# A hybrid decoder layer: the preparation and inverse of a block's delta rule moved into its own input projection

## The chip, the cores and the metric

One core of a Trainium2 chip runs the whole layer. The time is device microseconds (us) of one execution; the kernel before took 2666.4 us (median of three runs, 2665.94 to 2672.2).

## The reference

`x` is 2048 tokens of 1024 float32 channels; 16 meta tokens stand ahead of them. One layer:

```python
h = rmsnorm(x, norm1_g);  proj = h @ w_in            # 3608 columns: q, k, v, gates, decays
# four delta-rule heads (dk = dv = 128), after a causal conv of 4 taps, silu and l2norm of q and k:
a = (k * beta) @ k.T * decay;  m = I + strict_lower(a)
u, w = solve(m, v * beta), solve(m, k * beta * exp(gc))
v_new = u - w @ S;  o = (q * exp(gc)) @ S + (q @ k.T * decay) @ v_new
S = S * exp(gc[-1]) + (k * exp(gc[-1] - gc)).T @ v_new   # state, from chunk to chunk
# four GLA heads (dk = 64, dv = 128): the same with a decay per channel and no solve
o = rmsnorm(o) * silu(gate)                          # both groups
x = x + concat(o_dn, o_gla) @ w_out
x = x + square(relu(rmsnorm(x, norm2_g) @ w_up)) @ w_down;  out = rmsnorm(x, final_norm_g)
```

## The kernel before, in words

Products are made in float32 as three products of rounded halves (`mm3`, L117 to L120: high x high, low x high, high x low), into PSUM banks of 128 x 512. The tokens come in four blocks of 512 (`b` = 0 to 3), each of four chunks of 128 for the scan.

The program has these parts, in the order it is written:

- `phase_a(b)`: the input projection of block b, eight groups of four banks named `pa`, 96 matmuls for each group and pass over the banks: first a token group (`wtk[0]`: decays and the first part of GLA's values), three convolution groups (k, q, v), the GLA q and k group, and three token groups (values and gates). VectorE evacuates, makes the convolution (`cy`), the gates (`gth`) and the polynomial of log1p. Results go to DRAM (`qkv_d`, `gate_d`, `gla_d`, `gcr_d`).
- `scan_block(b)`: for the four chunks `dn_pre` (transposes of k and q, norms, `kdt`, `U`, `at`), then `dn_inverse` of the four `U` together: the 32 x 32 blocks on the diagonal go through DRAM (`inv_u`) into one tile `inv_v` of 64 partitions, 60 VectorE instructions invert them, and they go back the same way. Then for each chunk `gla`, `dn_levels` (the inverse of the whole 128 x 128 from its diagonal, matmuls `pr`, `pp`) and `dn_rec` (the delta rule proper, `pv`, `pks`, `py`, `po`, `pu`); `flush_mix` transposes results (`pmix`) and stores them in `mix_d`. A chunk's chain goes back and forth between PE and VectorE, each step on the one before; the state `S` links the chunks.
- `wo_block(b)`, in `tail_part`: the output projection of a block, two halves of four banks `pc`, 192 matmuls; residual, a sum of squares on GpSimd (`tot`), and `token_scale` (`pf`, `pfb`), whose result the norm uses at once.
- `layer1`, `layer2`: the MLP, two blocks at a time, by a Strassen scheme of seven products (`p`).

The order of the instructions on each engine is set by a scheduler at build time, which takes the parts' order in the program as priority and lets later parts fill an engine. So `phase_a(b + 1)` fills PE while `scan_block(b)` runs, and the output projections fill it during the last scan. `tc.high_priority(offset=n)` puts instructions n places earlier in that priority. Each engine then runs its own queue in order; a wait of an instruction holds all behind it. All transfers are issued on SyncE (SP), in order too. Tiles of a tag share `bufs` buffers in turn. Of the page's names, `b`, `x` and `tot` are the output projections' tiles.

The lines that set the order of the scan:

```python
scan_meta()
for b in range(NB):
    if b + 1 == NB:
        wstack.close()
    scan_block(b)
    if b + 1 < NB:
        phase_a(b + 1, ka)
tail_part(kc)
```

## Time and profile before

| what | value |
|---|---|
| runs | 2665.94, 2666.4, 2672.2 us |
| profiled execution | 2671.58 us, span of its instructions 2668.7 us |
| mean granted clock of PE | 0.959 |
| PE busy | 2464.6 us, 92% |
| VectorE (DVE) busy | 1871.9 us, 70% |
| ScalarE (ACT) busy | 1147.0 us, 43% |
| GpSimd (POOL) busy | 536.3 us, 20% |
| last input projection matmul starts | 919.2 us into the span |
| first MLP matmul starts | 1308.4 us |

Busy is the union of an engine's instructions. Matmuls overlap, so a busy PE can still be slowed: the granted clock says so, 1.00 being full speed and 0.50 half. The bracket at the end of a timeline row says how long the engine was idle before the instruction and what ended it. The row of a window has the time in which each engine was busy, with the number of its instructions.

### The profile page before, as it was taken

To read this page: it belongs to the slowest core of one execution; us is meant where nothing else is said; L and a number is where in the kernel's file an instruction comes from. 1 tells how busy PE (TensorE), PEld (TensorE's weight loads), DVE (VectorE), ACT (ScalarE), POOL (GpSimd) and SP (SyncE) were. 2 spreads that over 40 slices of the span, in tenths; PEclk is the share of its full clock that TensorE was granted. 3 is DMA by queue.
4 is the path that set the end of the run, shared out by engine and by line. 5 is a ranking of instruction groups with operands and counts; after the bars stand their busy time and mean duration, and the time that the engine had idled before them with its cause. 6 is when DMAs were issued, how large, how long until landed. Compare 5 with 4: busy or idle time off the path is not lost.

```text
span 2668.7 us, 36615 instructions
## 1 busy us (share of the span) xinstructions
PE 2464.6 (92%) x12810; PEld 2029.9 (76%) x12810; DVE 1871.9 (70%) x3377; ACT 1147.0 (43%) x2241; POOL 536.3 (20%) x408
## 2 busy tenths in 40 slices
PE   8998899989998999685999999999969999899997
PEld 6788688868877877574788887778757888788776
DVE  4776896796589676856576666677778666557765
ACT  4345345533444444333354544433354454444433
POOL 2124233342333223231111110000111111100002
PEclk9999999999999999796999999999989999999999
DMA  5266355535645584461444447567527444656644
GB/s 178 95 205 200 110 191 178 179 132 167 188 129 178 169 273 144 142 190 52 142 157 144 143 156 285 188 215 231 165 81 266 148 157 144 209 187 210 214 135 137
DMA packets 292304, 454.73 MB, mean 170 GB/s; under 512 B 44544, under 2 KB 147544, under 8 KB 292120
## 3 DMA queue, kind: packets, MB, share of 16 engines
q1 hardware_dynamic: 292120, 452.41, 52.6%
q8 instruction: 100, 1.64, 0.2%
q14 instruction: 84, 0.69, 0.1%
HBM read 329.58 MB, written 122.72 MB: 169 GB/s over the span
## 4 chain that ended last, share of the span: by engine, by line
PE 66%; DVE 18%; DMA 8%; issue 3%; ACT 2%; POOL 2%; SPq 1%; DVEq 0%; POOLq 0%; ACTq 0%
PE p L119 15%; PE p L118 15%; PE p L120 15%; PE pa L118 3%; PE pa L119 3%; PE pa L120 3%; DVE cy L425 2%; PE pc L118 1%; PE pc L119 1%; PE pc L120 1%; DVE wlo L103 1%; DVE inv_v L575 1%; DMA gcb<-gcr_d 1%; DVE inv_t L569 1%; DMA gl<-gla_d 1%
## 5 line engine op out<-in xcount | busy, mean ns | idle before, releaser
L119 PE MATMUL p<-bl,w7h 128*128 128x512 f32 x832 | 322.7, 398 | 8.4 <-DVE bl L967 8.3
L120 PE MATMUL p<-bh,w7l 128*128 128x512 f32 x832 | 319.9, 399 | 0.0
L966 ACT CAST w7h<-s 128x1024 fp32r<-128x1024 f32 (+1 forms) x128 | 120.6, 942 | 347.4 <-PE p L119 293.0
L102 ACT CAST whi<-wraw 128x1024 fp32r<-128x1024 f32 (+1 forms) x160 | 154.7, 967 | 241.4 <-PE pa L120 79.3
L118 PE MATMUL p<-bh,w7h 128*128 128x512 f32 x832 | 228.9, 403 | 14.5 <-ACT bh L966 12.4
L880 POOL TENSOR_TENSOR tot<-tot,sqk 128x512 f32<-128x512 f32 (+1 forms) x56 | 79.2, 1414 | 734.5 <-ACT sqk L879 725.7
L103 POOL TENSOR_TENSOR wlo<-wraw,whi 128x780 fp32r<-128x780 f32 (+1 forms) x64 | 147.2, 2301 | 361.4 <-ACT whi L102 265.5
L118 PE MATMUL pa<-hh,whi 128*128 128x512 f32 x512 | 208.7, 408 | 4.9 <-ACT whi L102 2.6
L119 PE MATMUL pa<-hl,whi 128*128 128x512 f32 x512 | 206.2, 403 | 0.0
L967 DVE TENSOR_TENSOR w7l<-s,w7h 128x1024 fp32r<-128x1024 f32 (+1 forms) x128 | 140.6, 1098 | 93.1 <-ACT w7h L966 88.4
L120 PE MATMUL pa<-hh,wlo 128*128 128x512 f32 x512 | 194.4, 404 | 9.6 <-POOL wlo L103 8.2
L118 PEld LDWEIGHTS p<-bh,w7h 128*128 128x128 f32 x832 | 159.7, 192 | 54.8 <-ACT bh L966 13.5
L967 DVE TENSOR_TENSOR w7l<-w,w7h 128x1024 fp32r<-128x1024 f32 (+1 forms) x96 | 102.1, 1063 | 134.7 <-ACT w7h L966 134.3
L119 PEld LDWEIGHTS p<-bl,w7h 128*128 128x128 f32 x832 | 158.1, 190 | 47.5 <-DVE bl L967 10.4
L120 PEld LDWEIGHTS p<-bh,w7l 128*128 128x128 f32 x832 | 157.4, 189 | 39.3
L119 PE MATMUL pa<-wlo,hh 128*128 128x390 f32 x512 | 180.4, 355 | 3.2 <-POOL wlo L103 1.9
L118 PE MATMUL pa<-whi,hh 128*128 128x390 f32 x512 | 167.6, 357 | 14.5 <-ACT hh L113 9.9
L120 PE MATMUL pa<-whi,hl 128*128 128x390 f32 x512 | 174.1, 348 | 0.5 <-DVE hl L114 0.5
L967 DVE TENSOR_TENSOR bl<-br,bh 128x1024 fp32r<-128x1024 f32 (+2 forms) x144 | 148.2, 1031 | 35.1 <-ACT bh L966 35.1
L966 ACT CAST bh<-br 128x1024 fp32r<-128x1024 f32 (+2 forms) x144 | 123.7, 859 | 87.6 <-PE p L120 49.3
L103 DVE TENSOR_TENSOR wlo<-wraw,whi 128x1024 fp32r<-128x1024 f32 (+1 forms) x96 | 113.9, 1186 | 67.0 <-ACT whi L102 66.7
L1067 POOL TENSOR_TENSOR q<-r 128x512 f32<-128x512 f32 x32 | 57.7, 1803 | 495.7 <-ACT r L1066 452.2
(381 smaller groups left out, 6197.5 us busy)
## 6 DMA issues: line engine op xcount, KB each, us to landing
br<-sq_d SPq DMA_DIRECT2D x208, 256.0 KB, 3.6
w<-in_dn_dram SPq DMA_DIRECT2D x96, 512.0 KB, 4.7
wraw<-in_wch_dram SPq DMA_DIRECT2D x64, 512.0 KB, 3.6
w<-in_up_dram SPq DMA_DIRECT2D x64, 512.0 KB, 3.7
sq_d<-q SPq DMA_DIRECT2D x128, 256.0 KB, 2.3
wraw<-in_wtk_dram SPq DMA_DIRECT2D x64, 390.0 KB, 3.9
sq_d<-c SPq DMA_DIRECT2D x96, 256.0 KB, 2.8
wraw<-in_wo_dram SPq DMA_DIRECT2D x32, 512.0 KB, 4.1
```

What stands on the lines that cost most here:

```text
L102: A.copy(out=hi[:, :, 0:n], in_=raw[:, :, 0:n])
L103: eng.tensor_tensor(out=lo[:, :, 0:n], in0=raw[:, :, 0:n], in1=hi[:, :, 0:n].bitcast(F32), op=ALU.subtract)
L118: T.matmul(o, lhsT=ah, rhs=bh, start=first, stop=False)
L119: T.matmul(o, lhsT=ah, rhs=bl, start=False, stop=False)
L120: T.matmul(o, lhsT=al, rhs=bh, start=False, stop=last)
L425: V.scalar_tensor_tensor(out=y, in0=raw[:, q : q + TB], scalar=convw[:, m, q : q + 1], in1=y, op0=ALU.mult, op1=ALU.add)
L569: V.tensor_tensor(out=t, in0=vv[:, 0:c, c : c + 1].broadcast_to([L, c, n]), in1=vv[:, c : c + 1, c + 1 : w].broadcast_to([L, c, n]), op=AL ...
L575: V.tensor_tensor(out=vv[:, 0:c, c + 1 : w], in0=vv[:, 0:c, c + 1 : w], in1=t, op=ALU.add)
L880: eng.tensor_tensor(out=tot, in0=tot, in1=sq, op=ALU.add)
L966: A.copy(out=hi, in_=x)
L967: V.tensor_tensor(out=lo, in0=x, in1=hi.bitcast(F32), op=ALU.subtract)
L1067: G.tensor_tensor(out=q12, in0=u, in1=r5, op=ALU.add)
```

## The change

- A new function `ahead(b, also)` makes a block's four `dn_pre` and its `dn_inverse`, at a high priority; `phase_a(b)` calls it (`mid`) after its three convolution groups, before its last four groups. With b > 0 the last chunk (`scan_chunk(b - 1, 3)`) of the block before goes with it. The other three chunks stand ahead of `phase_a(b)`; block 3's four chunks come after it.
- `kdt`, `U` and `at` of all chunks go to DRAM when made (three shared buffers, tag `pre`), and are loaded for their chunk. `dn_inverse` reads its diagonal blocks from `u_d` in DRAM straight into `inv_v` and writes them back there.
- log1p of the delta rule's decays (`whole`) is made in one go, not in steps between the projection's groups.
- In the output projections the sums of squares are added on VectorE, and `token_scale` of a block is made between the two halves of the next block (`between`), of the last block in the first group of `layer1`.

The order the scheduler makes, at three places. PE, from the last matmul of the third output block (`pc`) to the first of the fourth, before (`py` to `pmix` are the delta rule of a chunk, `pr5` starts one):

```order
L120 MATMUL pc_12128<-mxh_11970,wlo_12222 128x512
L669 MATMUL py_10458<-nkv_10444,U_9976 128x128 x4
L679 MATMUL pu_10474<-vs_10463,kdt_9963 128x128 x4
L597 MATMUL pr5_10610<-wt_10606,U_10045 32x32 x8
L679 MATMUL pu_10688<-vs_10677,kdt_10032 128x128 x4
L597 MATMUL pr5_10824<-wt_10820,U_10114 32x32 x8
L679 MATMUL pu_10902<-vs_10891,kdt_10101 128x128 x4
L597 MATMUL pr5_11038<-wt_11034,U_10183 32x32 x8
L679 MATMUL pu_11116<-vs_11105,kdt_10170 128x128 x4
L821 MATMUL pmix_11150<-ident_69,mix_11033 128x128 x4
L118 MATMUL pc_12351<-mxh_12304,whi_12357 128x512
```

The same place on PE in the changed kernel:

```order
L120 MATMUL pc_12307<-mxh_12117,wlo_12401 128x512
L610 MATMUL pr5_11209<-wt_11205,U_11203 32x32 x8
L685 MATMUL py_11275<-nkv_11261,U_11203 128x128 x4
L695 MATMUL pu_11291<-vs_11280,kdt_11253 128x128 x4
L837 MATMUL pmix_11325<-ident_69,mix_11202 128x128 x4
L118 MATMUL pc_12505<-mxh_12458,whi_12511 128x512
```

(Rows between those shown are left out.) Four delta rules, the first in its second half, stood between the two blocks; now one does. The first delta rule of block 3 starts after 192 of the 768 `pc` matmuls, the second after 324, the third after 466.

PE where the sum of squares of the second output block is used, before:

```order
L120 MATMUL pc_11751<-mxh_11597,wlo_11845 128x512
L856 MATMUL pf_11896<-ones_70,tot_11601 128x1 x4
L871 MATMUL pfb_11905<-dg_11906,ones_70 128x128
L118 MATMUL pc_11975<-mxh_11928,whi_11981 128x512
L119 MATMUL pc_11975<-mxl_11929,whi_11981 128x512
```

The sum of the same block in the changed kernel, in the middle of the third block (`pp5`, `pr6` to `pks` are a chunk's delta rule):

```order
L120 MATMUL pc_12125<-mxh_12117,wlo_12219 128x512
L867 MATMUL pf_12273<-ones_70,tot_11746 128x1 x3
L630 MATMUL pr6_11016<-wt_10985,U_10983 64x64 x4
L681 MATMUL pks_11049<-S_182,kg_11045 128x128 x4
L882 MATMUL pfb_12282<-dg_12283,ones_70 128x128
L118 MATMUL pc_12304<-mxh_12075,whi_12310 128x512
```

`pf` and `pfb` stood between two blocks, right behind the last sum; now 96 `pc` matmuls lie between, with scan work around them.

VectorE amid the inverse (`inv_t`, `inv_v`) of the second block, before:

```order
L167 SCALAR_TENSOR_TENSOR l1p_6430<-l1p_6430,gle_6427 128x512
L425 SCALAR_TENSOR_TENSOR cy_6434<-craw_6412,convw_147,cy_6434 128x512
L569 TENSOR_TENSOR inv_t_4931<-inv_v_4930 64x238
L575 TENSOR_TENSOR inv_v_4930<-inv_v_4930,inv_t_4931 64x17x14
L569 TENSOR_TENSOR inv_t_4931<-inv_v_4930 64x240
L575 TENSOR_TENSOR inv_v_4930<-inv_v_4930,inv_t_4931 64x16x15
```

The inverse of the same block in the changed kernel:

```order
L635 COPY U_4357<-pp6_4396 64x4x64
L589 TENSOR_TENSOR inv_v_4164<-inv_v_4164,inv_t_4165 64x19x12
L671 TENSOR_TENSOR nkv_4415<-pv_4410,nkh_1473 128x512
L583 TENSOR_TENSOR inv_t_4165<-inv_v_4164 64x234
L358 SCALAR_TENSOR_TENSOR gth_5086<-gth_5086,tok_5072 128x390
L682 TENSOR_TENSOR nkv_4415<-nkv_4415,pks_4423 128x512
L589 TENSOR_TENSOR inv_v_4164<-inv_v_4164,inv_t_4165 64x18x13
L687 TENSOR_TENSOR vs_4434<-py_4429,brk2_1476 128x512
```

The inverse stood among the convolution and log1p of the next block's projection; now it stands among the gates of its own and the delta rule of the last chunk before.

The diff, cut to its core:

```diff
+    u_d, at_d, kdt_d = [[dp.tile([128, 4, 128], F32, name=f"{n}_d{c}") for c in range(NCH)] for n in ("u", "at", "kdt")]
+    u_m = dp.tile([NMETA, 4, NMETA], F32, name="u_m")
...
-    def phase_a(b, kc, late=None):
+    def phase_a(b, kc, late=None, mid=None):
...
+        def whole(job):
+            try:
+                while True:
+                    next(job)
+            except StopIteration as end:
+                return end.value
...
-            l = yield from log1p(e[:p], p, [nt, 4], f"l1p_s{nt}")
+            l = whole(log1p(e[:p], p, [nt, 4], f"l1p_s{nt}"))
...
+        mid()
...
-            kqv = bp.tile([128, 12, 128], F32, name="kqv", tag="kqv", bufs=2)
+            kqv = bp.tile([128, 12, 128], F32, name="kqv", tag="kqv", bufs=3)
...
-        nkh = bp.tile([128, 4], F32, name="nkh", tag="nkh", bufs=5)
+        nkh = bp.tile([128, 4], F32, name="nkh", tag="nkh", bufs=9)
         V.tensor_scalar(out=nkh[:p], in0=ss[:p, 0:4], scalar1=0.5, scalar2=2 * EPS, op0=ALU.mult, op1=ALU.add)
         V.tensor_tensor(out=nkh[:p], in0=nkh[:p], in1=rk[:p, 0:4], op=ALU.mult)
-        brk2 = bp.tile([128, 4], F32, name="brk2", tag="brk2", bufs=5)
+        brk2 = bp.tile([128, 4], F32, name="brk2", tag="brk2", bufs=9)
...
-            rq = bp.tile([128, 4], F32, name="rq", tag="rq", bufs=5)
+            rq = bp.tile([128, 4], F32, name="rq", tag="rq", bufs=9)
...
-        kdt = b2k("kdt", "kdt", 4)
+        kdt = b2k("kdt", "pre", 3) if c is not None else b2k("kdt", "kdt", 1)
...
-        U = b2k("U", "U", 4)
+        U = b2k("U", "pre", 3) if c is not None else b2k("U", "U", 2)
...
-            at = b2k("at", "at", 4)
+            at = b2k("at", "pre", 3)
             V.tensor_tensor(out=at, in0=h4(pqk), in1=gm, op=ALU.mult)
-            r["at"] = at
+            for x, d in ((kdt, kdt_d), (U, u_d), (at, at_d)):
+                nc.sync.dma_start(out=d[c], in_=x)
+            U = kdt = None
...
-        d1 = dp.tile([L, w, w], F32, name=f"inv_u{name}")
-        d2 = dp.tile([L, w, w], F32, name=f"inv_v{name}")
+        v = bp.tile([64, 1024], F32, name="inv_v", tag="inv_v", bufs=1)
+        tm = bp.tile([64, 256], F32, name="inv_t", tag="inv_t", bufs=1)
+        vf = v[:L, 0 : w * w]
+        vv = vf.rearrange("l (s c) -> l s c", s=w)
+        blocks = []
...
-                nc.sync.dma_start(out=d1[l0 : l0 + 4].rearrange("h s c -> s h c"), in_=r["U"][qs, :, qs])
-        v = bp.tile([64, 1024], F32, name="inv_v", tag="inv_v", bufs=1)
-        tm = bp.tile([64, 256], F32, name="inv_t", tag="inv_t", bufs=1)
-        vf = v[:L, 0 : w * w]
-        vv = vf.rearrange("l (s c) -> l s c", s=w)
-        nc.sync.dma_start(out=vv, in_=d1)
+                blocks.append(((u_m if meta else u_d[r["c"]])[qs, :, qs].rearrange("s h c -> h s c"), vv[l0 : l0 + 4]))
+        if meta:
+            nc.sync.dma_start(out=u_m, in_=rs[0]["U"][0:w, :, 0:w])
+        for d, x in blocks:
+            nc.sync.dma_start(out=x, in_=d)
...
-        nc.sync.dma_start(out=d2, in_=vv)
-        for i, r in enumerate(rs):
-            for q in range(nq):
-                l0 = (i * nq + q) * 4
-                qs = slice(w * q, w * (q + 1))
-                nc.sync.dma_start(out=r["U"][qs, :, qs], in_=d2[l0 : l0 + 4].rearrange("h s c -> s h c"))
+        for d, x in blocks:
+            nc.sync.dma_start(out=d, in_=x)
+        if meta:
+            nc.sync.dma_start(out=rs[0]["U"][0:w, :, 0:w], in_=u_m)
...
-            U = vt = r["U"]
+            U = vt = r["U"] = b2k("U", "U", 2)
+            nc.sync.dma_start(out=U, in_=u_d[r["c"]])
...
-            kqv = bp.tile([128, 12, 128], F32, name="kqv", tag="kqv", bufs=2)
+            kqv = bp.tile([128, 12, 128], F32, name="kqv", tag="kqv", bufs=3)
             nc.sync.dma_start(out=kqv, in_=qkv_d[b][:, :, t * 128 : (t + 1) * 128])
+            at, kdt = b2k("at", "at", 1), b2k("kdt", "kdt", 1)
+            nc.sync.dma_start(out=at, in_=at_d[c])
+            nc.sync.dma_start(out=kdt, in_=kdt_d[c])
         else:
-            kqv = kqv_m
+            kqv, kdt = kqv_m, r["kdt"]
...
-                T.matmul(h4(po)[:, h, :], lhsT=r["at"][:, h, :], rhs=vs[:, h, :], start=False, stop=True)
+                T.matmul(h4(po)[:, h, :], lhsT=at[:, h, :], rhs=vs[:, h, :], start=False, stop=True)
         pu = ps("pu")
         for h in range(4):
-            T.matmul(h4(pu)[:, h, :], lhsT=r["kdt"][:p, h, :], rhs=vs[:p, h, :], start=True, stop=True)
+            T.matmul(h4(pu)[:, h, :], lhsT=kdt[:p, h, :], rhs=vs[:p, h, :], start=True, stop=True)
...
-    def scan_block(b):
-        rs = [dn_pre(4 * b + t) for t in range(4)]
-        flush_mix()
-        dn_inverse(rs)
-        for t, r in enumerate(rs):
-            c = r["c"]
-            for i in (1, 0):
-                gate = b2k("gate", "gate", 2)
-                nc.sync.dma_start(out=gate.rearrange("p h c -> p (h c)"), in_=gate_d[b][t][:, i * 512 : (i + 1) * 512])
-                mix = b2k("mix", "mix", 2)
-                if i == 0:
-                    dn_levels([r])
-                    dn_rec(r, gate, mix, False)
-                else:
-                    gla(c, gate, mix)
-                flush_mix()
-                late_mix.append((c, i, mix))
-        if b == NB - 1:
+    def scan_chunk(b, t):
+        r = ready[b][t]
+        c = r["c"]
+        for i in (1, 0):
+            gate = b2k("gate", "gate", 2)
+            nc.sync.dma_start(out=gate.rearrange("p h c -> p (h c)"), in_=gate_d[b][t][:, i * 512 : (i + 1) * 512])
+            mix = b2k("mix", "mix", 2)
+            if i == 0:
+                dn_levels([r])
+                dn_rec(r, gate, mix, False)
+            else:
+                gla(c, gate, mix)
             flush_mix()
+            late_mix.append((c, i, mix))
...
-        def wo_block(b, x):
+        def wo_block(b, x, between=None):
...
-            tot = e512("tot", "tot", 1)
+            tot = e512("tot", "r", 4)
             for half in range(2):
+                if half and between is not None:
+                    between(mm)
...
-                    square_sum(tot, t, k == 0, sqt)
-            rb = token_scale([tot], mm, *small)
-            if x:
-                norm(x, rb)
-            else:
-                t = e512("x", "r", 4)
-                A.copy(out=t, in_=rb)
-                nc.sync.dma_start(out=rb_d[b], in_=t)
+                    square_sum(tot, t, k == 0, sqt, V)
+
+            def scale(bk):
+                rb = e512("rb", "r", 4)
+                A.copy(out=rb, in_=token_scale([tot], bk, *small))
+                if x:
+                    norm(x, rb)
+                else:
+                    nc.sync.dma_start(out=rb_d[b], in_=rb)
+
+            return scale
...
-        wo_block(0, b11 + b21)
-        wo_block(1, b12 + b22)
-        wo_block(2, None)
-        wo_block(3, None)
+        sc = wo_block(0, b11 + b21)
+        sc = wo_block(1, b12 + b22, sc)
+        sc2 = wo_block(2, None, sc)
+        sc3 = wo_block(3, None, sc2)
...
-                if later and g in (0, 1):
-                    later[g]()
+                if later and g < len(later):
+                    later[g](bank)
...
-                    def go():
+                    def go(bk):
...
-        layer1(raw_s, x7, None)
+        layer1(raw_s, x7, [sc3])
...
-    phase_a(0, ka, late_consts)
+    def ahead(b, also=()):
+
+
+        def go():
+            with tc.high_priority(offset=1000):
+                ready[b] = [dn_pre(4 * b + t) for t in range(4)]
+                dn_inverse(ready[b])
+                for t in also:
+                    scan_chunk(b - 1, t)
+
+        return go
+
+    ready = {}
+    phase_a(0, ka, late_consts, ahead(0))
     scan_meta()
     for b in range(NB):
-        if b + 1 == NB:
+        if b + 1 < NB:
+            for t in range(3):
+                scan_chunk(b, t)
+            phase_a(b + 1, ka, None, ahead(b + 1, (3,)))
+        else:
             wstack.close()
-        scan_block(b)
-        if b + 1 < NB:
-            phase_a(b + 1, ka)
+            for t in range(4):
+                scan_chunk(b, t)
+            flush_mix()
```

## Prediction

> **What bounds the kernel now.** I read the page first (engines, slices), then the idle time of PE by stretch, then the timeline where PE stands still, and last VectorE and the landings.
>
> The page's first two parts:
>
> ```profile
> PE 2464.6 (92%) x12810; PEld 2029.9 (76%) x12810; DVE 1871.9 (70%) x3377; ACT 1147.0 (43%) x2241; POOL 536.3 (20%) x408
> ...
> PE   8998899989998999685999999999969999899997
> ...
> PEclk9999999999999999796999999999989999999999
> ```
>
> PE bounds the whole, so a change gains only where PE stands or is slowed. A slice is 66.7 us; slices 17 to 19 of 40 (1067 to 1267 us) read 6, 8, 5 with a granted clock of 0.7 to 0.9. That is the end of the scan beside the output projections. I cut it by the first and last matmul of each projection block (`pc`), from the last input projection matmul (919.4) to the first of the MLP (1308.4). Columns: PE, PEld, DVE, ACT, POOL, then clock, DMA share, GB/s.
>
> ```profile
> 919.40:933.30 13.90, 11.33 (x87) 10.11 (x87) 8.28 (x19) 6.34 (x19) 0.23 (x1) 0.75 0.85 266
> 933.30:1000.30 67.00, 65.13 (x454) 52.64 (x454) 47.14 (x105) 30.23 (x72) 20.19 (x22) 1.00 0.84 272
> 1000.30:1014.00 13.70, 11.44 (x87) 10.25 (x86) 11.38 (x27) 8.13 (x27) 8.54 (x9) 0.75 0.42 145
> 1014.00:1089.20 75.20, 71.33 (x458) 59.96 (x457) 47.00 (x123) 30.05 (x116) 21.15 (x18) 0.98 0.56 164
> 1089.20:1106.60 17.40, 2.38 (x11) 2.17 (x11) 15.28 (x37) 8.67 (x21) 10.07 (x8) 0.59 0.71 230
> 1106.60:1167.00 60.40, 52.78 (x269) 42.47 (x269) 40.40 (x83) 14.85 (x21) 10.85 (x9) 0.89 0.39 121
> 1167.00:1254.50 87.50, 57.65 (x531) 49.48 (x529) 53.15 (x148) 31.25 (x107) 23.26 (x28) 0.78 0.34 105
> 1254.50:1308.40 53.90, 47.34 (x193) 38.11 (x194) 38.85 (x57) 23.81 (x35) 5.43 (x4) 0.89 0.47 150
> ...
> sum 389.00, PE 319.38 PEld 265.19 DVE 261.48 ACT 153.32 POOL 99.72; mean PE 39.92 PEld 33.15 DVE 32.68 ACT 19.17 POOL 12.46
> ```
>
> Call them S0 to S7. S1, S3, S5 and S7 hold one block of 192 `pc` each; between them no projection matmul runs. The worst are S4, where PE waits for a sum of squares, and S6, where three whole chunks and the end of another run with no projection beside them. The timeline of PE there:
>
> ```profile
> 1088.46 0.40 PE L118 MATMUL pc<-mxh,whi 128*128 128x512 f32 x1
> 1088.70 0.39 PE L119 MATMUL pc<-mxl,whi 128*128 128x512 f32 x1
> 1088.92 0.40 PE L120 MATMUL pc<-mxh,wlo 128*128 128x512 f32 x1
> 1102.14 1.86 PE L856 MATMUL pf<-ones,tot 128*128 128x1 f32 x8 [12.82 <-POOL tot L880]
> 1106.21 0.79 PE L871 MATMUL pfb<-dg,ones 128*128 128x128 f32 x2 [2.20 <-ACT dg L870]
> ...
> 1118.63 0.49 PE L871 MATMUL pfb<-dg,ones 128*128 128x128 f32 x2 [1.71 <-DVE dg L868]
> ...
> 1166.97 1.05 PE L669 MATMUL py<-nkv,U 128*128 128x128 f32 x8
> ...
> 1205.08 0.62 PE L597 MATMUL pr<-wt,U 32*32 32x32 f32 x16 [2.07 <-DVE wt L589]
> ...
> 1220.71 0.27 PE L761 MATMUL pA<-qi,ki 64*64 64x64 f32 x1
> ...
> 1227.43 0.44 PE L597 MATMUL pr<-wt,U 32*32 32x32 f32 x16 [1.50 <-DVE f_u L87]
> ...
> 1244.88 1.01 PE L821 MATMUL pmix<-ident,mix 128*128 128x128 f32 x4 [3.28 <-DVE mix L637]
> 1254.52 2.07 PE L118 MATMUL pc<-mxh,whi 128*128 128x512 f32 x4 [8.63 <-ACT mxh L113]
> ```
>
> **Prices from these rows.** One `pc` matmul starts 0.23 after the last (1088.46, 1088.70, 1088.92), so a block costs PE 192 x 0.23 = 44.2. An uncovered chunk takes 1227.43 - 1205.08 = 22.3: about 17.7 the delta rule (with its 2.07 wait, up to `pA` at 1220.71), the rest GLA. A covered chunk: S1 has 67.0 - 44.2 = 22.8 beside its `pc`, and the program has two chunks there; so 11.4 each, which I split 7.4 (delta rule) and 4.0 (GLA).
>
> **The change, part by part.** All the matmuls stay, so I count only waiting: a stretch, less 0.23 for each `pc`, less the covered price of the scan in it.
>
> 1. *Block 3's preparation and inverse, and the last chunk of block 2, go into the last input projection.* The order puts only one delta rule behind the third output block instead of three and a half chunks. S6 now: 87.5 - (3 x 11.4 + 3.7 for the half + 2 for `pf`, `pfb`) = 47.6 of waiting. Then: 1254.5 - 1227.4 + about 2 for its first wait = 29.1, less 7.4 of work = 21.7 (the link through `mix_d` to the last block stays). Gain 25.9. The chunks that leave it lie beside the second and third output blocks in the order: 88 of PE over three chains of 22.3 = 67, so they are covered.
>
> 2. *Sums of squares used later, and added on VectorE.* `pf` comes half a block after its sum, so PE no longer waits at a block's end. S4 holds about 2.4 of work in 17.4: 15.0 waiting; I leave 3 for the operands of the next block: gain 12. S5: 60.4 - 44.2 - 3.7 (half a delta rule) - 1 = 11.5, in which the 1.71 above and 5.9 for the norms ahead of its first products lie; I leave 4: gain 7.5. S2: 13.7 less 5 of GLA and `pf` = 8.7; I leave 4: gain 4.7. The 28 added sums on VectorE:
>
> ```profile
> L880 POOL TENSOR_TENSOR tot<-tot,sqk x26: 1262/1294/3398, 979.8 to 1308.8; 128x512 f32<-128x512 f32 x26
> ...
> L925 DVE TENSOR_TENSOR b<-b,pc x16: 672/680/689, 972.7 to 1097.1; 128x512 f32<-128x512 f32 x16
> ```
>
>    28 x 0.68 = 19 us on an engine with 261.5 busy of 389; the order sets most of them behind the evacuations of the banks, so I take 0 and at most 28 x 0.68 / 4 = 5 where a bank waits behind one.
>
> 3. *S0.* A whole delta rule now runs at the end of the last input projection instead of a half: 17.7 - 7.4 = 10.3 waiting against 13.9 - 3.7 - 4.0 = 6.2: loss 4.
>
>    Parts 1 to 3: 25.9 + 12 + 7.5 + 4.7 - 4 = 46. S3 keeps its price: what it has beyond 44.2 and a chunk is 75.2 - 44.2 - 11.4 = 19.6 for four preparations, paid in the projection instead.
>
> 4. *Ends of the other input projections.* The end of block 0's is now bare: its preparation is done earlier and its inverse runs still. The next projection needs a gate store and a load of `xk` (they share buffers):
>
> ```profile
> gate_d<-gth SPq DMA_DIRECT2D x32, 195.0 KB, 3.6
> xk<-in_xT_dram SPq DMA_DIRECT2D x32, 256.0 KB, 4.7
> ...
> inv_v<-inv_u SPq DMA_DIRECT2D x4, 256.0 KB, 4.3
> ...
> kqv<-qkv_d SPq DMA_DIRECT2D x16, 768.0 KB, 6.2
> ...
> 458.62 0.45 PE L118 MATMUL pa<-whi,hh 128*128 128x390 f32 x1 [1.19 <-ACT hh L113]
> ```
>
>    3.6 + 4.7 less some 2 that overlap the last matmuls = 6 lost; at 458.62 the scan filled such an end and 1.19 was left, so the bounds are 1 and 8. At the next two ends the last chunk's delta rule runs with the inverse's instructions between its own on VectorE: 38 of 60 in the order, at 22.8 / 60 = 0.38 each (next fence) 14 longer, of which I put a third outside cover: 4 each, 8 (bounds 0 and 28).
>
> 5. *VectorE.* The inverse now lies beside the gate projections, not beside convolutions:
>
> ```profile
> 249.10:305.20 56.10, 19.26 (x60) 1.00 0.46 138
> 527.00:621.80 94.80, 22.77 (x60) 0.95 0.45 143
> ...
> 540.00:600.00 60.00, 49.85 (x201) 37.81 (x199) 57.83 (x128) 23.02 (x33) 25.09 (x9) 0.95 0.39 132
> 300.00:320.00 20.00, 14.64 (x62) 10.28 (x61) 15.69 (x30) 6.90 (x11) 6.13 (x4) 0.77 0.64 167
> ```
>
>    The first two rows are inverses (VectorE's part alone), the last two the whole core: at 540 to 600 VectorE is busy 57.8 of 60 and PE idle 10.2; at 300 to 320 PE is idle 5.4. I take half of 15.6, 8 gained (bounds 0 and 16): the convolutions meet the scan's chunks instead, which also use VectorE.
>
> 6. *Stores and loads.* 88 more transfers (24 per block, less 2), `U`, `at`, `kdt` out and back. Loads of 256 KB land in 4.3 to 4.7 us. The order issues a chunk's `at` and `kdt` while the chunk before runs, 11 to 22 us ahead, and `U` of all but a block's first chunk too; the first chunk's `U` has the rest of a projection over it. Cost 0; with the cover gone, 4.3 for each of 16 chunks. `log1p` of the 16 scalars in one go, the third `kqv` buffer and `kdt`, `U`, `at` sharing three buffers: 0, all beside other work.
>
> Sum: 46 - 6 - 8 + 8 = 40. Against the profiled execution (2671.6, with a span of 2668.7) this gives 2631.6; the median of the runs is 5.2 lower, 2666.4, so 2626.
>
> **A rule of the Trainium skill.** The rows give PE idle in S0 to S7 as 389.0 - 319.4 = 69.6, yet my waiting sums to 6.2 + 8.7 + 15 + 11.5 + 47.6 and S7's 53.9 - 44.2 = 9.7, that is 98.7; the clock column (0.59 in S4, 0.78 in S6) has the difference. The Trainium skill, "TensorE: Matmul & The Clock Gate", section "HAM oscillation — how this bites in real kernels", says that a pause of PE beyond about 3.4 us also halves the clock of what follows. This case's clock column agrees: 1.00 in S1, 0.59 where PE waited 12.82. By idle time alone parts 1 to 3 would be worth 46 x 69.6 / 98.7 = 32; by the rule 46.
>
> **Rivals.**
> - *VectorE gives more* (chance 0.15): all 16 of part 5, and the 14 of part 4 not paid: 40 + 8 + 14 = 62, 2604. For it: 57.83 of 60. Against: a bare chunk needs VectorE too, 53.2 in S6 for three and a half.
> - *The inverse of block 3 is late* (0.13): the delta rule of block 3 stands behind one output block (44 + about 22 of S0 + 4 GLA = 70); inverses took 56.1 to 94.8. At 94.8 PE stops for 25: 40 - 25 = 15, 2651. For it: VectorE between. Against: the 94.8 was with VectorE full.
> - *No change* (0.07): the convolutions and three chunks now share VectorE for each of blocks 1 to 3. At 53.2 / 3.5 = 15 of VectorE for a chunk, nine chunks that lose 4.4 each take the 40 back: 2666.
> - *Slower* (0.10): the reloads are on the chain, `U` above all, since PE takes its instructions in order. 16 x 4.3 = 69 less 40 = 29 slower, 2695; it decides from 40 / 16 = 2.5 us a chunk. Against: the loads of `kqv`, 6.2, are in the chain today and not among the waits of the PE rows of S6. The Trainium skill, "DMA: Bandwidth & Descriptors", section "Anatomy of one DMA — SWDGE (gpsimd) path", gives about 2.0 us of fixed cost for each DMA, mostly its completion, on another path than this one; two of them for each round trip would be an estimated 64 for 16 chunks, if nothing covered them.
>
> **Numbers.** My forecast has 0.55 (own range 2610 to 2642), the rivals as above. The range reaches from 2598, somewhat under the first rival, to 2656, past the second, and leaves out the last two. A change under 0.3% (8 us) can't be told from none here: faster 0.83, same 0.07, slower 0.10.
>
> **What would show it.** Right: only one delta rule between the third output block and the last; no wait for `tot` of over 3 us; the clock from the end of the input projections to the MLP above 0.9; that part some 95 shorter, since beside the 46 about 50 of scan work moves ahead of it (four preparations, two and a half delta rules, three of GLA). Wrong: waits of `pr` or `wt` for loads of `U`; a wait at the first `pr` of block 3; an input projection longer by more than its added scan work (11.4 a chunk).

## The result, and the profile after

The changed kernel is slower: 2688.9 us (median of four runs, 2683.54 to 2689.82) against 2668.93 (four runs, 2665.94 to 2672.2), a ratio of 1.007 with an interval of 1.005 to 1.0091. The forecast was 2626 and "faster". The page after, its span, engines and slices of PE with the granted clock:

```profile
span 2688.0 us, 36763 instructions
...
PE 2468.2 (92%) x12810; PEld 2034.4 (76%) x12810; DVE 1900.8 (71%) x3405; ACT 1145.8 (43%) x2243; POOL 498.0 (19%) x380
...
PE   8958999899989997996999999999969999899997
...
PEclk9979999899999998997999999999989999999998
```

The low slices 17 to 19 of before (6, 8, 5) are gone but for one 6. In their place slice 3 (134 to 202 us, inside block 0's projection) reads 5 with a clock of 0.7. The busy time by stretch shows the same (columns: PE, PEld, DVE, ACT, POOL, clock, DMA share, GB/s). The first two rows are the second half of the first input projection, the next three the ends of the first three; the last seven answer to S0 to S7 (S4, 0.2 us now, has no row):

```profile
138.60:187.30 48.70, 20.07 (x129) 17.26 (x128) 24.46 (x73) 19.01 (x92) 9.46 (x6) 0.67 0.69 216
187.30:256.00 68.70, 67.48 (x380) 62.08 (x376) 51.93 (x142) 26.50 (x58) 19.32 (x15) 0.94 0.58 177
256.00:267.40 11.40, 0.17 (x1) 0.00 (x1) 7.41 (x23) 6.05 (x12) 1.83 (x1) 0.71 0.77 245
513.80:528.60 14.80, 10.20 (x69) 9.39 (x68) 10.26 (x22) 3.14 (x6) 2.56 (x1) 0.77 0.74 219
770.80:780.60 9.80, 4.75 (x40) 4.03 (x39) 8.44 (x20) 2.94 (x5) 2.71 (x1) 0.95 0.77 208
1014.90:1041.00 26.10, 13.19 (x119) 11.58 (x117) 16.52 (x49) 7.96 (x22) 3.66 (x4) 0.67 0.97 325
1041.00:1091.50 50.50, 48.78 (x236) 39.22 (x234) 39.35 (x96) 18.73 (x35) 6.41 (x8) 1.00 0.68 225
1091.50:1092.00 0.50, 0.50 (x18) 0.34 (x17) 0.00 (x0) 0.50 (x1) 0.00 (x0) 1.00 0.92 340
1092.00:1162.00 70.00, 65.68 (x433) 53.61 (x430) 51.70 (x94) 29.55 (x63) 12.88 (x12) 0.98 0.61 200
1162.00:1237.70 75.70, 70.66 (x447) 59.16 (x445) 47.60 (x105) 26.34 (x67) 10.56 (x13) 0.93 0.51 161
1237.70:1266.00 28.30, 13.45 (x111) 11.31 (x109) 19.62 (x41) 14.00 (x33) 3.95 (x3) 0.67 0.34 112
1266.00:1329.80 63.80, 53.15 (x208) 42.24 (x209) 42.10 (x63) 25.16 (x38) 2.02 (x1) 0.85 0.42 133
```

The part from the last input projection matmul to the MLP took 389 us and now takes 315 (1014.9 to 1329.8). The part ahead took 919 and now takes 1015. The MLP is unchanged. "Waiting" below is a stretch less the interval that each of its matmuls has at full clock in the kernel before, so it holds idle time and lost clock. Each size is from one profiled execution of a kernel, and another fair choice of the intervals moves it by 2 or 3 us.

The largest new wait is in the first row. PE there, in the changed kernel's timeline:

```profile
138.36 0.40 PE L120 MATMUL pa<-hh,wlo 128*128 128x512 f32 x1
142.96 1.08 PE L498 MATMUL pk<-ident,kqv 128*128 128x128 f32 x4 [4.20 <-DMA kqv<-qkv_d]
...
150.97 1.60 PE L541 MATMUL pkk<-kqv 128*128 128x128 f32 x8 [1.82 <-ACT sq L511]
155.79 2.08 PE L550 MATMUL pqk<-kqv 128*128 128x128 f32 x8 [3.22 <-DVE U L544]
...
165.98 1.16 PE L541 MATMUL pkk<-kqv 128*128 128x128 f32 x8 [2.60 <-DVE U L544]
...
167.96 1.50 PE L264 MATMUL pmeta<-wraw,hm 128*32 128x256 f32 x24
186.25 1.08 PE L264 MATMUL pmeta<-wraw,hm 128*32 128x256 f32 x8 [16.79 <-DMA wraw<-in_wch_dram]
187.32 0.79 PE L118 MATMUL pa<-hh,whi 128*128 128x512 f32 x1
```

Block 0's four preparations run with no projection matmul beside them, and then PE stands 16.79 us for weights. PE is idle for 28.6 us of this stretch: 16.8 for the weights, and 11.8 in four waits of the preparations themselves (4.20, 1.82, 3.22 and 2.60), which nothing fills, since the order puts no projection matmul among them. SyncE's queue at that time shows what is issued when (start, time of the issue, transfer):

```profile
164.90 4.82 SPq L663 DMA_DIRECT2D at<-at_d  x1
...
170.28 1.70 SPq L479 DMA_DIRECT2D gcb<-gcm_d  x1
...
173.26 4.71 SPq L661 DMA_DIRECT2D kqv<-qkv_d  x2
178.07 3.61 SPq L98 DMA_DIRECT2D wraw<-in_wch_dram  x1
...
239.94 8.76 SPq L592 DMA_DIRECT2D u_d<-inv_v  x16
248.80 1.48 SPq L359 DMA_DIRECT2D gate_d<-gth  x3
...
252.51 6.15 SPq L98 DMA_DIRECT2D wraw<-in_wtk_dram  x4
...
263.26 0.90 SPq L185 DMA_DIRECT2D xk<-in_xT_dram  x2
```

The queue issues in order. `at` and `kqv` of scan chunks that run much later stand ahead of the weights (`wraw`) that PE needs at 168. The queue is not the only hold on them. They are the group's fourth load, and `wraw` has three buffers; block 0's `pmeta` matmuls read them, and these stand behind the preparations too, at 167.96. So the load could not have been issued before about 168 by an empty queue either; x13 below shows that case. From 239.94 the inverse's 16 stores take 8.76 us, and the gate stores and `xk` of the next projection come behind them; the first matmul of that projection starts at 267.40.

### The profile page after: what moved, and what is told of

It reads as the page before. It is cut to its first block, busy times and chain, and to the rows that moved or that the text cites. A ratio compares the mean times of both kernels' runs of the same rounds, so it can differ in the third digit from the quotient of the medians.

```text
span 2688.0 us, 36763 instructions
## 1 busy us (share of the span) xinstructions
PE 2468.2 (92%) x12810; PEld 2034.4 (76%) x12810; DVE 1900.8 (71%) x3405; ACT 1145.8 (43%) x2243; POOL 498.0 (19%) x380
## 4 chain that ended last, share of the span: by engine, by line
PE 52%; DVE 7%; DMA 3%; issue 1%; ACT 1%; SPq 1%; POOL 0%; DVEq 0%; POOLq 0%; ACTq 0%
PE p L119 15%; PE p L118 15%; PE p L120 15%; PE pc L120 2%; PE pc L118 2%; PE pc L119 1%; DMA br<-sq_d 1%; DVE bl L983 1%; DVE b L954 0%; DVE wlo L103 0%; DMA gcb<-gcr_d 0%; DMA xr<-xs_d 0%; DMA gl<-gla_d 0%; SPq L592 0%; DMA mixk<-mix_d 0%
## 5 line engine op out<-in xcount | busy, mean ns | idle before, releaser
L118 PE MATMUL pa<-whi,hh 128*128 128x390 f32 x512 | 173.7, 361 | 17.9 <-ACT hh L113 17.5
L891 POOL TENSOR_TENSOR tot<-tot,sqk 128x512 f32<-128x512 f32 (+1 forms) x28 | 37.9, 1354 | 625.7 <-ACT sqk L890 624.5
```

The costliest lines, as they stand in the source:

```text
L118: T.matmul(o, lhsT=ah, rhs=bh, start=first, stop=False)
L891: eng.tensor_tensor(out=tot, in0=tot, in1=sq, op=ALU.add)
```

## Experiments

| run | median us | ratio to before | second projection starts | last input projection ends | MLP starts |
|---|---|---|---|---|---|
| before | 2668.9 | | 228.3 | 919.2 | 1308.4 |
| changed | 2688.9 | 1.0050 to 1.0091 | 267.4 | 1014.8 | 1329.8 |
| x1 no move | 2705.6 | 1.0118 to 1.0159 | 228.3 | 919.7 | 1346.9 |
| x2 block 0 in the old place | 2666.3 | 0.9977 to 1.0003 | 226.3 | 948.5 | 1307.9 |
| x3 late sums alone | 2675.1 | 1.0010 to 1.0032 | 227.2 | 916.8 | 1314.5 |
| x4 two kqv | 2684.0 | 1.0040 to 1.0077 | 263.9 | 1011.2 | 1327.8 |
| x5 block 0 later | 2669.1 | 0.9983 to 1.0005 | 243.7 | 994.5 | 1306.1 |
| x6 scale at once | 2677.1 | 1.0015 to 1.0039 | 260.9 | 1004.7 | 1311.4 |
| x7 at, kdt on chip, no move | 2669.5 | 0.9991 to 1.0015 | 228.2 | 904.8 | 1310.9 |
| x8 = x5 and x6 | 2668.6 | 0.9987 to 1.0009 | 248.5 | 1002.8 | 1312.8 |
| x9 = x5, old sums | 2686.4 | 1.0038 to 1.0074 | 244.6 | 995.4 | 1320.4 |
| x10 = x8, at on chip | 2658.9 | 0.9931 to 0.9970 | 243.3 | 995.3 | 1302.0 |
| x11 = x10, last chunk first | 2643.9 | 0.9886 to 0.9929 | 246.3 | 997.0 | 1292.7 |
| x12 = x11, plain priority | 2686.6 | 1.0046 to 1.0081 | 260.4 | 1018.4 | 1330.9 |
| x13 trips on GpSimd | 2680.0 | 1.0024 to 1.0050 | 268.1 | 1011.9 | 1319.6 |
| x14 inverse's transfers on ScalarE | 2691.6 | 1.0061 to 1.0092 | 265.9 | 1021.1 | 1331.6 |
| x15 = x11 and x14 | 2694.6 | 1.0068 to 1.0099 | 257.4 | 1021.2 | 1330.4 |
| x16 few transfers | 2661.3 | 0.9953 to 0.9980 | 259.6 | 1002.3 | 1302.3 |
| x17 = x11 and x16 | 2645.9 | 0.9892 to 0.9920 | 241.9 | 990.0 | 1291.6 |

Ratios are taken against runs of the kernel before that were made beside each kernel's (medians of 2668.4 to 2670.7). The last three columns are positions in one profiled execution. Kernels with the same order up to there still differ: the last input projection ends at 1014.8 in the changed kernel and at 1004.7 in x6, which is 10 us apart, so differences of kernels are taken from the medians.

### The parts of the change one at a time

x1: the changed kernel, with each block's preparation and inverse (`prepare(b)`) put back behind its projection.

```diff
-    phase_a(0, ka, late_consts, ahead(0))
+    phase_a(0, ka, late_consts, nothing)
...
+        prepare(b)
+        for t in range(4):
+            scan_chunk(b, t)
```

> The changed kernel's parts without the move: U, at and kdt go through DRAM, the softplus of g is one piece, the sums of squares are used late, but each block's preparation and inverse stand where the kernel before has them, behind the block's input projection and ahead of its chunks. First theory (the move is what costs: it puts preparations, inverses and a delta rule bare into the input projections, block 0's above all): this kernel is within 8 us of the kernel before, 2661 to 2677, and its input projections end within 10 us of before's 919. Rival (the round trips through DRAM cost by themselves, 23 MB more traffic, U, at and kdt back on the chain of each chunk): 2680 or more, with waits of the first matmuls of a chunk for the loads of U, at or kdt of over 2 us each, sixteen times.

2705.6: the rival on the time, and the first theory falls. But the loads don't stretch the chain of the chunks: two delta rules in a row start 24.3 us apart here (first fence) and 24.2 in x3, which has no round trips (second fence, both the timeline of PE). VectorE waits for a load of `U` three times (4.55, 3.67 and 1.89), and PE behind it 1.17 us at most, where the rival had sixteen waits of over 2.

```profile
1187.45 0.44 PE L610 MATMUL pr<-wt,U 32*32 32x32 f32 x16
1211.77 0.44 PE L610 MATMUL pr<-wt,U 32*32 32x32 f32 x16 [2.07 <-DVE wt L602]
```

```profile
1154.60 0.64 PE L597 MATMUL pr<-wt,U 32*32 32x32 f32 x16 [5.68 <-DVE wt L589]
1178.80 0.44 PE L597 MATMUL pr<-wt,U 32*32 32x32 f32 x16 [2.07 <-DVE wt L589]
```

So the move itself gains 17 us over x1, and what it had to carry, the round trips, costs more.

x2: only block 0 goes back (`prepare(0)` behind `scan_meta()`).

> The changed kernel with block 0's preparation and inverse back behind block 0's input projection; blocks 1 to 3 keep the move. First theory (block 0's move costs some 31 us in the first input projection: 28.9 us in which TensorE is frozen while loads jam at 139 to 187 us, and a bare end at 256 to 267): the first input projection ends near 215 to 230 instead of 267; the whole is 20 to 30 us under the changed kernel, 2658 to 2668, less what the scan's lost lead gives back in the tail (in the program's order chunk (3,0)'s delta rule then stands at the second output block instead of at its start). Rival (the waits of block 0 are only moved: the same preparation costs as much behind its projection, and the lead is lost too): 2685 to 2705.

As the first theory had it: 23 us less than the changed kernel, and the tail longer by 44 (359 against 315), since the scan starts later.

x3: the kernel before with the late sums alone (the scale `sc` of a block is made between the halves of the next).

```diff
-                    square_sum(tot, t, k == 0, sqt)
-            rb = token_scale([tot], mm, *small)
+                    square_sum(tot, t, k == 0, sqt, V)
...
+        sc = wo_block(1, b12 + b22, sc)
```

> The kernel before with one part of the change alone: the sums of squares of an output block are added on VectorE, and the scale that comes of them is computed in the next block. The prediction's second part gave this 24 us (2645). First theory (the tail before was set by the chain of the scan, which ran on other engines while TensorE waited for the sums; without that wait TensorE waits for the scan instead): 2661 to 2677, no wait for the sums left, and as much more waiting for the scan of block 3. Rival (the waits for the sums were TensorE's own and the prediction's step was right): 2640 to 2650.

The first theory: 7 us slower. The windows of x3 that answer to S6 and S7:

```profile
1148.60:1252.70 104.10, 63.11 (x584) 54.11 (x582) 56.69 (x156) 31.69 (x108) 21.05 (x27) 0.75 0.31 94
1252.70:1314.40 61.70, 51.10 (x208) 41.07 (x209) 42.13 (x64) 25.25 (x38) 2.02 (x1) 0.88 0.43 137
```

The waits for `tot` went and S6 grew from 87.5 to 104.1: its end, 1252.7, is where it was (1254.5). The last block grew from 53.9 to 61.7.

x7: x1 with `at` and `kdt` kept on chip (four buffers each, and two kqv for the room), so that only `U` makes the trip.

> The run without the move again, but at and kdt stay in on-chip memory; only U goes through DRAM: two of three round trips are gone, some 17 MB of 23. In the order of instructions the preparation of block 3 still stands bare at the end of the second output block, as in the run without the move, since the order is fixed at build time. First theory now (the 30 us that the round trips add to the late-sums kernel come from that order: with the loads in it the inverse and each chunk stand later among the matmuls of the projections, until block 3's preparation stands bare in the tail): 2690 to 2708, close to the run without the move's 2706, with the same bare stretch ahead of the third output block. Rival (traffic and loads cost by themselves, at about 1.3 us for each MB): 2680 to 2688.

Both theories miss: 36 us under x1. The bare stretch ahead of the third output block is there, but 38.5 us long against 64.4, and the projections end 15 us earlier. So the two trips, with the buffers that change beside them, cost 36 us there; how much by the order that the scheduler makes with them and how much on the chip was not separated, since a transfer added can shift that order.

### Block 0

x4: two buffers for kqv (`bufs=3` to `2`), which takes one of the loads from ahead of the weights.

> The changed kernel with two buffers for kqv instead of three, so that one load of a later scan chunk less stands ahead of the weight load in SyncE's queue in block 0's projection. If the freeze of TensorE at 139 to 187 us comes from loads of later chunks that stand ahead of the weights in that queue, it gets some 5 us shorter (the one load took 4.7 us to issue), and the whole 0 to 8 us shorter, 2678 to 2688. If the freeze comes from the traffic of the preparation itself, or from VectorE, no change there (2684 to 2692), and the later chunks' loads of kqv may come later and cost.

5 us less, and the stretch from 138 to 187 shrinks by 2: in the direction of the loads, too small to tell by itself.

x5: block 0's call of `mid()` one group later.

```diff
-        mid()
+        if b:
+            mid()
         group(I["wch"][3], 512, True, evac_g, done_g, 512 if meta else 0, meta_g)
+        if meta:
+            mid()
```

> The changed kernel with one call moved: block 0's preparation and inverse come one group of columns later in the first input projection (behind the fourth group of channels instead of ahead of it), so that this group's weights are asked for ahead of the preparation's loads and its matmuls can run between them. First theory (what block 0's move costs is the 28.9 us in which TensorE stands for weights that wait behind the preparation's and later chunks' loads, and the lead of the scan is worth what it gave in the tail): the wait at the first `pa` of the fourth group goes under 8 us, the first input projection ends 15 to 30 us earlier than the changed kernel's 267, the tail stays within 10 us of its 315, and the whole is 2655 to 2675. Rival (the preparation costs as much wherever it stands in that projection, by its own chain and the traffic): the wait turns up at another group or at the projection's end; 2683 to 2695.

20 us less: the wait at the fourth group is gone, the second projection starts 24 us earlier, the tail is 312. Part of the rival is seen too: 10.45 us of waiting for weights turn up in a later group. PE's idle time from the first to the last matmul of this projection is 9.8 us before, 34.1 in the changed kernel and 15.6 here, where the preparations stand among projection matmuls. Of these 18.5 us, some 9 are the preparations' own waits, mostly covered now (11.8 to 2.7), and 6 are the weights (16.79 to 10.45).

### The sums and their scale

x6: `sc2(mm)` straight behind the third output block.

> The changed kernel with one call moved: the scale of the third output block is computed straight behind that block, as in the kernel before, instead of between the halves of the fourth. There it stands beside the delta rule of the last chunk, for which TensorE waits 21 us anyway. If the last output block's 63.8 us against 53.7 before come from that scale (its 14 matmuls of 3.9 us and waits of 2.79, 0.23, 0.38 and 0.68 us between the halves), this block takes 54 to 57 us and the whole is 6 to 9 us shorter: 2680 to 2683. If they come from the sums of squares on VectorE, no change (2686 to 2691).

12 us less by the medians; in the profile the last block takes 55.4 (before 53.9, changed 63.8), and the rest lies ahead of 1005 us, where nothing was changed and the order is the same: a difference of executions. The timeline of the changed kernel shows the cost that went:

```profile
1298.13 0.95 PE L867 MATMUL pf<-ones,tot 128*128 128x1 f32 x8
1301.86 0.80 PE L882 MATMUL pfb<-dg,ones 128*128 128x128 f32 x2 [2.79 <-ACT dg L881]
1302.90 0.79 PE L118 MATMUL pc<-mxh,whi 128*128 128x512 f32 x1 [0.23 <-DVE x L938]
1303.49 0.63 PE L119 MATMUL pc<-mxl,whi 128*128 128x512 f32 x1
1303.91 0.63 PE L120 MATMUL pc<-mxh,wlo 128*128 128x512 f32 x1
```

A pause of 2.79, and then matmuls 0.43 apart instead of 0.23 for 6 us, as the clock column of S7 (0.85) has it.

x8: this and x5 together.

> Both repairs at once: block 0's preparation one group later, and the third output block's scale straight behind that block. If the two costs are separate (block 0's loads ahead of the weights; the scale's 14 matmuls and waits between the halves of the last block, which here too can lie beside the last delta rule, for which TensorE waits 17.8 us bare), it is 6 to 9 us under the run with block 0 later alone (2669): 2659 to 2664, faster than the kernel before by 0.2 to 0.4%. If the last delta rule no longer covers the scale: 2667 to 2672.

2668.6: no gain over x5. The last block is 4.1 shorter (57.7), the last delta rule ahead of it 3.1 longer (27.0 against 23.9). Where the scan is further ahead, its end no longer hides the scale.

x9: x5 with the output blocks of the kernel before (sums and scale at each block's end).

> The run with block 0's preparation later, with the output blocks as in the kernel before: sums of squares on GpSimd and VectorE as there, and each block's scale straight behind it, so that TensorE waits for `tot` at each block's end. In the order of instructions the last delta rule now ends by the end of the second output block instead of behind the third, since the scan fills those waits. First theory (the scan's chain and the work of TensorE set the tail; a wait for a sum taken away is a wait for the scan later, and late sums give nothing even where the scan is ahead): within 8 us of 2669, 2658 to 2677, with waits of 10 to 20 us for `tot` back and the bare delta rule ahead of the last block gone. The prediction's second part (late sums take 24 us of waits out of the tail): 2685 to 2697.

17 us slower than x5: the prediction's second part is right here, and the theory formed after x3 is not. PE waits for the sums again, in its timeline:

```profile
1188.51 1.87 PE L870 MATMUL pf<-ones,tot 128*128 128x1 f32 x8 [3.13 <-POOL tot L894]
...
1268.80 1.87 PE L870 MATMUL pf<-ones,tot 128*128 128x1 f32 x8 [9.38 <-POOL tot L894]
```

So late sums cost 7 us where the scan is late (x3) and give 17 where it is ahead.

### Round trips, order and priority

x10: x8 with `at` on chip.

```diff
-            at = b2k("at", "pre", 3)
+            at = b2k("at", "at", 5)
...
-            for x, d in ((kdt, kdt_d), (U, u_d), (at, at_d)):
+            for x, d in ((kdt, kdt_d), (U, u_d)):
```

> Both repairs, and `at` stays in on-chip memory (five buffers; kqv has two instead of three for the room), so that one of the three round trips, 8 MB, is gone, with nearly the same order of matmuls in the tail. If the round trips cost by themselves (36 us went with `at` and `kdt` both kept, where the preparation stood in the old place): 8 to 18 us under the run with both repairs, 2644 to 2655. If they cost there only through the place that the order gives to block 3's preparation: no change, 2657 to 2666.

10 us less with nearly the same order, and the first version faster than the kernel before. x10 changes two more things: two buffers instead of three for `kqv` and for `pre`. In x4 the `kqv` buffer alone gave 5 us, so one trip of 32 transfers costs at most about 10 us here, and perhaps half of it.

x11: the last chunk of each block with its own, higher priority, and the scale between the halves again.

```diff
+            with tc.high_priority(offset=2000):
                 for t in also:
                     scan_chunk(b - 1, t)
```

> The run with `at` kept and block 0 later, but the third block's scale again between the halves of the last block as in the changed kernel, and the last chunk of each block with a higher priority (2000 against 1000). In the order of instructions the scan now ends within the third output block, so no delta rule stands bare ahead of the last block (27.5 us long in the run with `at` kept, in which TensorE waits some 18). If the tail goes by how far the scan is ahead when the last input projection ends: 12 to 20 us under that run's 2659, 2639 to 2647. Rival (what the order gains there comes back as waits for the delta rules amid the output blocks, as their own chain of 18 to 24 us each sets their pace): 2652 to 2664, with waits of over 2 us at `pr`, `pp` and `py` of block 3 between `pc`.

2643.9, 15 us under x10 and the fastest: 9.6 us are left bare ahead of the last block, against 27.5.

x12: no raised priority anywhere (`offset=0`).

> As the run with the last chunk first, but with no raised priority at all for the preparations, the inverses and the last chunks. The order is nearly the same from block 1 on; in block 0 the preparations stand some 20 to 40 matmuls later, among the weights' own. If the raised priority matters only by the order it gives: within 6 us of that run. Rival (the raised priority also puts loads ahead of weights in SyncE's queue, and that is what block 0's wait came from): 5 to 12 us less than that run.

Both fall: 43 us slower than x11, with nearly the same order on PE. SyncE's queue at the end of block 0 in x12, and the same in x11 behind it:

```profile
242.31 9.45 SPq L596 DMA_DIRECT2D u_d<-inv_v  x16
...
255.37 1.85 SPq L185 DMA_DIRECT2D xk<-in_xT_dram  x4
```

```profile
228.81 8.87 SPq L596 DMA_DIRECT2D u_d<-inv_v  x16
...
242.06 0.46 SPq L185 DMA_DIRECT2D xk<-in_xT_dram  x1
```

With the priority the inverse's stores are issued 13.5 us earlier, while the projection still runs, and are out of the way of `xk`. PE is idle 21.96 us there in x12 and 10.01 in x11, so 12 of the 43. The rest, 17 of it in the tail (312 against 296), wasn't traced to a cause.

### SyncE's queue

Up to the MLP SyncE issues 783 transfers in the kernel before, in 340 us, and 870 in the changed one, in 404 (sums over its rows; with its semaphore instructions 399 and 483).

x13: the changed kernel with the round trips issued on GpSimd (`nc.sync` to `G` at their stores and loads).

> The changed kernel with the round trips of U, at and kdt issued on GpSimd's queue instead of SyncE's; the order of matmuls stays nearly the same. Theory (the round trips cost by their place in SyncE's queue, which works in order: up to 1330 us it spends 483 us on issuing, against 399 before, and weights, `xk` and `mixk` stand behind): the wait for weights at 139 to 187 us gets 5 to 15 us shorter, the whole 8 to 20: 2669 to 2681. Rival (the transfers cost by their bytes, whichever queue issues them): no change, 2684 to 2694. Second rival: the wait of each store holds up GpSimd's halves of the weights (`wlo`), slower than 2694.

9 us less, at the weak end of the theory. The wait for the weights shrank as the theory had it, from 16.79 to 8.71, but the stretch that is 138 to 187 in the changed kernel did not get shorter (48.6 against 48.9). PE in x13, and SyncE's queue behind it:

```profile
169.26 2.79 PE L264 MATMUL pmeta<-wraw,hm 128*32 128x256 f32 x24 [5.08 <-DVE at L552]
180.76 1.08 PE L264 MATMUL pmeta<-wraw,hm 128*32 128x256 f32 x8 [8.71 <-DMA wraw<-in_wch_dram]
```

```profile
167.34 0.53 SPq L661 DMA_DIRECT2D kqv<-qkv_d  x1
170.44 2.81 SPq L98 DMA_DIRECT2D wraw<-in_wch_dram  x1
```

Here the queue stands idle for 2.5 us until `pmeta` frees a buffer, issues the weights at once, and PE still waits 8.71. By that, an estimate from these two waits, about 8 of the 16.79 are the queue's and 8.7 are the load's, behind the preparations. And the preparations took longer by as much (the 5.08 for `at`). So a lighter SyncE queue gives nothing in this stretch here, and 4 to 5 us in x14 and x16 below (43.9 and 45.3 long); x5, which changes the order, takes it apart.

x14: the inverse's 32 transfers a block on ScalarE (`A.dma_start`), and x15: the same in x11.

> The changed kernel with the 32 small transfers of each block's inverse (`inv_v` from and to `u_d`) issued on ScalarE's queue instead of SyncE's. In SyncE's queue the 16 stores take 8.8 us from 240 us on, with the gate stores and `xk` of the next projection behind them, and at 1006 and 1019 us eight of the loads stand ahead of the first `mixk`. Theory (queue): block 0's projection ends in 1 to 6 us instead of 11.4, the start of the output blocks takes 12 to 18 us instead of 26, and the whole is 10 to 25 us shorter: 2664 to 2679. Rival (bytes and waits as such): 2684 to 2694. Second rival: ScalarE, which waits for the transfers' sources in order, delays `whi` and `hh`: slower than 2694.

> The run with the last chunk first (2644), with the inverse's transfers on ScalarE's queue. Theory (queue): what is left of waits at the ends of the projections there (10.3, 10.4, 15.7 and 15.2 us) shrinks by 1 to 4 us each: 2630 to 2640. Rival (these ends are set by the gates, whose buffers `xk` shares, and not by the queue): 2640 to 2650.

x14 is 3 us slower than the changed kernel, x15 51 slower than x11. The ends of the projections did get shorter in x14 (7.7, 10.3, 7.7 and 14.3 us against 11.6, 15.0, 10.0 and 26.2), but two of the four projections themselves got longer, by 9 and 14 us. ScalarE's timeline in x15, at the stores:

```profile
234.34 9.22 ACTq L596 DMA_DIRECT2D u_d<-inv_v  x16
243.62 1.54 ACT L351 ACTIVATE tok<-pa,rt 128x390 f32<-128x390 f32 x3 [10.21 <-DMA u_d<-inv_v]
```

The issuing takes as long on this engine and holds up its evacuation of the banks. How much of the 51 us this makes was not traced: the end of block 0's projection is 12 us longer in x15 than in x11, and the tail 13.5.

x16: the same bytes in fewer transfers, on SyncE: one for each head over the four chunks (core of the diff).

```diff
-                blocks.append(((u_m if meta else u_d[r["c"]])[qs, :, qs].rearrange("s h c -> h s c"), vv[l0 : l0 + 4]))
+            ub = u_b[rs[0]["c"] // 4].rearrange("t (q r) -> (t q) r", q=4)[:, 0:16384].rearrange("l (s h c) -> l h s c", s=32, h=4)
+            blocks = [(ub[:, h, :, 0:32], vv[h:64:4]) for h in range(4)]
```

> The changed kernel with the inverse's transfers of a block in 4 loads and 4 stores instead of 16 and 16 (one for each head, over all four chunks; the same bytes, in a DRAM layout with a gap of 128 bytes for every 32 rows), still on SyncE's queue. Theory (the 16 stores' 8.8 us of issuing in SyncE's queue hold up the gates and `xk` of the next projection, `mixk` at the start of the output blocks, and the delta rule): stores take 2 to 4 us, and the whole is 8 to 20 us shorter, 2669 to 2681. In the order the scan gains 60 matmuls on the second output block too, worth up to 15 more. Rival (issuing takes as long for the same descriptors in fewer transfers, or the ends of the projections hang on the data): 2684 to 2694.

28 us less than the changed kernel, 0.3% faster than the kernel before. Its queue at block 0's end:

```profile
237.38 2.62 SPq L593 DMA_DIRECT2D u_b<-inv_v  x4
...
254.91 0.43 SPq L187 DMA_DIRECT2D xk<-in_xT_dram  x1
```

2.62 us for the bytes that took 8.76; up to the MLP 774 transfers and 355 us of issuing instead of 870 and 404. The ends take 9.7, 8.8, 9.0 and 17.3 us, 18 less in sum. The other 10 were not split; the order moved too, which the expectation had put at up to 15. The kernel before has as many small transfers of the inverse (64 stores and 64 loads of 16 KB), so this is a gain beside the change, not a cost of the change undone.

x17: this in x11.

> The fastest version so far (2644) with the inverse's transfers in 4 loads and 4 stores a block. In the order block 3's delta rules come 24 to 90 matmuls later and the last ends behind the third output block again, which would cost up to 18. Theory (queue): 2636 to 2652, with shorter ends of the first and third projections. Rival (the order's loss alone): 2652 to 2662.

2645.9, level with x11: the ends are not shorter there (12.3, 10.5, 15.5 and 13.2 against 10.4, 10.5, 15.8 and 15.3), and the last delta rule stands bare again (18.9 us). x11 and x17 are the fastest, 0.9% under the kernel before.

## Why the prediction was wrong, step by step

The forecast gained 40 us; the waiting grew by 21.5 (98.5 to 151.2 ahead of the tail, counted from the middle of the first projection, and 111.6 to 80.4 in the tail). The 61.5 between them are in the main four terms: 34.5 (block 0), 11.6 (part 5), 8 (part 3) and 8 (part 2).

- *Part 1 (S6): right.* Waiting 47.3 to 21.1, a gain of 26.2 for 25.9. One delta rule is left between the last two output blocks.
- *Part 2 (late sums): right in place and size, with a term and a condition left out.* Waiting in S1 to S5 went from 49.4 to 24.6, 24.8 for 24.2. But the scale of the third block was free inside S6 and now stands in the last block: 63.8 for 53.9, 8 of waiting that the sum did not have (S7; x6 takes 8.4 of it away). The condition: alone, the sums cost 7 (x3); they give 17 with the scan ahead (x9).
- *Part 3 (S0): mis-sized.* 4 forecast, 11.8 measured (4.7 to 16.5). `mixk` is issued at 1030, behind the inverse's loads, the gate stores and the scan's loads in SyncE's queue; with fewer transfers S0 is 17.3 long instead of 26.2 (x16, where the order moved too).
- *Part 4 (ends of the projections): right in sum.* 14 forecast, 14.5 measured (3.4, 6.5 and 4.6).
- *Block 0 inside its projection: the step that failed.* Part 4 priced block 0's end alone and part 6 set its stores and loads at 0, "all beside other work". From the middle of that projection to its end the waiting grew from 6.6 to 41.1, so 34.5. The cover named, "all beside other work", was the projection itself, and it was not there: the order put the four preparations where no projection matmul ran beside them (11.8 us of their own waits bare), and the weights of the next matmuls came late behind them (16.8 us), partly through the queue and partly through their buffers. x2 and x5, which move only this, give 23 and 20 back. How the 16.8 divide is an estimate only (x13).
- *Part 5 (VectorE): no gain.* 8 gained in the forecast; the waiting inside the other three projections grew by 3.6 (80.7 to 84.3), which is within what two executions differ by. What took the 8 was not measured.
- *Part 6 (trips at 0): wrong.* Up to 10 us for `at` (x10). The prediction asked when a load lands, and that was nearly right: of a block's chunks only the first waits, VectorE 3.00, 7.74 and 5.70 us for the `U` of blocks 1 to 3, since the inverse's stores are issued just ahead of that load. The longest, VectorE and then PE in the changed kernel:

```profile
829.99 0.71 DVE L602 STREAM_TRANSPOSE wt<-U 128x512 f32<-128x512 f32 x1 [7.74 <-DMA U<-u_d]
...
830.76 0.44 PE L610 MATMUL pr<-wt,U 32*32 32x32 f32 x16 [0.87 <-DVE wt L602]
```

PE loses 0.87 us there and nothing at the other two. The prediction did not ask what stands behind 87 more issues.

- *Rivals.* "Slower by reloads on the chain" ends near the measured time (2695) by luck and fails as a mechanism (x1's chunks, and the 0.87 above). The Trainium skill, "DMA: Bandwidth & Descriptors", section "Issuing engines are not separate DMA queues", says that issuing from several engines saves only the time to initiate a transfer, usually small beside the transfer. Here it was 8.76 us for 16 stores, which is not small in a queue that weights share; x16 issues them in 2.62.
- *The clock.* In the tail PE's idle time fell by 20 us (69.6 to 49.4) and the waiting by 31: part of the gain is clock, as the prediction had it. The mean clock there, 0.89 from the rows above, misses the "above 0.9".
- *Signs named.* Of the right ones, one delta rule is left and no wait for `tot` is left in the tail; the clock is 0.89 for "above 0.9", and the tail is 74 us shorter for "some 95". Of the wrong ones, two came true: `wt` waits for loads of `U` (which cost PE 0.87), and an input projection is longer by more than its added scan work (the second starts 39 us later, for preparations priced at 19.6).

## What to carry to other kernels

When a step is moved, list what it puts into each in-order queue at its new place, issues of transfers included, and who stands behind them: a load that lands in time for its own user can still be in the way of another's. An engine's own instructions are such a queue too: here the matmuls that free the weights' buffers stood behind the preparations. A wait of the bounding engine is worth its length only if what runs beside it is not itself the end of the stretch; ask first which chain ends last with the wait gone. Before a round trip through DRAM is written as many small transfers, look for a layout that makes it few.
